# Block sums of an MLP weight matrix: added on VectorE, or by accumulating transfers on GpSimd's queue during the RWKV part

## The chip, the cores and the metric

The kernel runs on one core of a Trainium2 chip. TensorE (PE) multiplies matrices; its weight loads have a row of their own in the profile (PEld). VectorE (DVE), ScalarE (ACT) and GpSimd (POOL) work on tiles in the core's memory, and SyncE (SP) issues most of the transfers. POOL and ACT can issue transfers too. The metric is the device time of one execution in microseconds (us), as the median of several runs. Lower is better.

## The reference

One layer of a hybrid decoder runs on 512 new prompt tokens and 64 sample tokens (8 sequences of 8), so 576 rows of width 1024. RWKV-7 time mixing and differential attention run on the same normalised input and are merged by gates; then comes an MLP with a squared ReLU:

```python
xn = rmsnorm(x, lp['g_mix'], NORM_EPS)
P = xn @ lp['w_in']
...
o_a, S = rwkv7_branch(Pr, S0, lp)
...
m = gate_a * (o_a @ lp['w_br_a']) + gate_b * (o_b @ lp['w_br_b'])
x = x + m @ lp['w_out']
hn = rmsnorm(x, lp['g_ffn'], NORM_EPS)
x = x + jnp.square(jax.nn.relu(hn @ lp['w_up'])) @ lp['w_down']
```

`w_up` is 1024 x 4096 and `w_down` 4096 x 1024. Everything is float32. The outputs are the final rows, the new keys and values, the RWKV states and the last normalised rows.

## The kernel before

Activations are kept transposed: 128 channels on the partitions, 576 tokens on the free axis, cut into two halves of 288. Weights come in blocks of 128 x 128. To keep float32 accuracy, each operand is split into a rounded half `hi` (made by ACT) and a rest `lo` (made by DVE), and each product is three matmuls: hi times hi, hi times the rest of the other operand, and the reverse.

`stream` (called through `dense` and `finish`, or held as a generator) does this for one column block of a weight: `load` brings its raw rows on SP's queue into a ring of three buffers (tag "raw"), `halve` splits them into rings "hi" and "lo" of three, then for each half of the tokens and each k three matmuls follow, and an eviction closes each half. One such triple is the unit that the change counts.

The stages are, in the order of the program: Q, K and V of four heads (`qkv`), attention (`prompt`, `sample`), then the RWKV part (`rwkv`, `chain`), whose small, dependent steps leave holes on PE. These are filled with streams from a list `waiting`, by `fill` and `take`: 14 shifted projections (`shifted`, tile names z), 16 gates (`gate`, g, two blocks of 8) and 8 blocks of the attention's output projection (`branch_b`, brb, of 8 triples each where the others have 16). A gate ends with the store of its result to `gt_d` (line 452). After that come the RWKV branch's output projection (bra), the product with `w_out` (wo), and the MLP.

POOL's work in the RWKV part consists of small steps inside the chain (the powers `nr` and `var`, the copy `nb`, clearing `ST` and `TT`, the masked products `vm`), one clearing per shifted stream (`Z`), and stores of results (`out_Sp`, `out_Ss`, `oa_d`). The load of the sample states `s0` on SP (line 859) reuses a buffer that such a store reads.

The first MLP product is done in pairs of column blocks (`up_pair`). Weights and activations are seen as 2 x 2 blocks, and seven block products in place of eight are formed from sums of blocks. Sums of the activations (`t1` to `t4`) are made once, while `w_out` runs. The sums of the weights are made anew for every pair: `s12` holds a21 + a22 and that minus a11; `s34` holds a11 - a21 and a12 minus the second of `s12`. These are four DVE additions of 128 x 512. Then `halve` splits `s12`, the first row, `s34` and a22. `down` multiplies with `w_down` between the pairs.

The order on each engine isn't written out by hand. A planner orders instructions by priority as their inputs become ready in its own model of time. `prio(FEED + ...)` puts loads and halvings ahead of everything else on their engines, and `prio(FILL + ...)` orders the matmuls. What the planner has put in a queue is then executed in that order, and an instruction that waits holds up those behind it on its engine.

Of the kernel before, what the change touches and what calls it, by code (L numbers as in the profile page):

```python
# [8 lines left out]
F32 = mybir.dt.float32  # L9
F32R = mybir.dt.float32r  # L10
I32 = mybir.dt.int32
AF = mybir.ActivationFunctionType
# [3 lines left out]
P = 128  # L16
# [9 lines left out]
DFF = 4096  # L26
# [15 lines left out]
def tile_hybrid_step(ctx, tc, xT, xsT, ktab, vtab, s0T, ptab, w_in, vecs, w2a2, g2, lamv,  # L42
                     w_bra, w_brb, w_out, w_up, w_down, cst, bias_p, bias_s,
                     yT, kTo, vTo, Sp, Ss, sh):
    nc = tc.nc
# [9 lines left out]
    ring = {"job": 0}  # L55

    def act(out, in_, func=AF.Copy, **kw):
        ring["act"] = AE.activation(out=out, in_=in_, func=func, **kw)  # L58

    def tt(out, a, b, op, eng=None):  # L60
        ins = (eng or VE).tensor_tensor(out=out, in0=a, in1=b, op=op)  # L61
        if eng is None:
            ring["tt"] = ins

    def stt(out, a, s, b, op0, op1):
        VE.scalar_tensor_tensor(out=out, in0=a, scalar=s, in1=b, op0=op0, op1=op1)
# [4 lines left out]
    def mm(out, lhsT, rhs, start=True, stop=True):  # L71
        ring["mm"] = PE.matmul(out=out, lhsT=lhsT, rhs=rhs, start=start, stop=stop)  # L72
        return ring["mm"]
# [9 lines left out]
    FEED, LATE, FILL = -1000000, 500000, 1000000  # L83

    @contextmanager
    def prio(at):
        was, tc.cur_priority = tc.cur_priority, at
        yield
        tc.cur_priority = was

    MUL, ADD, SUB, MAX = ALU.mult, ALU.add, ALU.subtract, ALU.max
# [20 lines left out]
    c = const.tile([P, C_END], F32, name="cst_sb")  # L112
# [41 lines left out]
    def stream(src, kt, xh, xl, spans, evac, name, raws=None, together=False, banks=None,  # L154
               keep=None):


        his, los = [], []
        n = min(kt, ring["piece"])
        if src is None:  # L160

            job = ring["job"] = ring["job"] + 1
            raws = []
            his, los = ([t[:, k] for k in range(kt)] for t in keep)
        else:
            job, raws = raws or load(src, kt, name)

        def halve(i):
            raw = raws[i]
            with prio(FEED + 1000 * job + 100 if banks is None else FEED + 1001 + 40 * i + job):  # L170
                if keep:
                    hi, lo = (t[:, i * n:(i + 1) * n] for t in keep)
                elif banks is None or i == 0:
                    hi = ring["pool"].tile([P, n, P], F32R, tag="hi", name=f"hi_{name}_{i}")
                    lo = ring["pool"].tile([P, n, P], F32R, tag="lo", name=f"lo_{name}_{i}")
                else:
                    hi, lo = (zp.tile([P, NT], F32R, tag=f"Pt{job - 1}", name=f"{half}_{name}_{i}", bufs=2)[
                        :, :n * P].rearrange("p (k w) -> p k w", k=n) for half in ("hi", "lo"))
                act(hi, raw)
                tt(lo, raw, f32(hi), SUB)  # L180
                his.extend(hi[:, k] for k in range(n))
                los.extend(lo[:, k] for k in range(n))
        for i in range(len(raws)):
            halve(i)
        pss = banks or [psd.tile([P, 512], F32, tag="d", name=f"ps_{name}_{i}") for i in range(len(spans))]
        order = [(k, i) for i in range(len(spans)) for k in range(kt)]
        for k, i in sorted(order) if together else order:
            t0, w = spans[i]
            ps = pss[i]
            rh, rl = (x[k][:, t0:t0 + w] if isinstance(x, list) else x[:, k, t0:t0 + w] for x in (xh, xl))  # L190
            yield 1000 * job
            mm(ps[:, :w], his[k], rh, start=(k == 0), stop=False)
            yield 1000 * job
            mm(ps[:, :w], his[k], rl, start=False, stop=False)
            yield 1000 * job
            mm(ps[:, :w], los[k], rh, start=False, stop=(k == kt - 1))
            if k == kt - 1:
                with prio(FEED + 1000 * job + 200 + 20 * i):
                    evac(ps[:, :w], t0, w)
# [63 lines left out]
    oa_d = tc.dram_tile([HB, P, NT], F32, name="oa_d")  # L263
    ob_d = tc.dram_tile([HB, P, NT], F32, name="ob_d")
    gt_d = tc.dram_tile([2 * KT, P, NT], F32, name="gt_d")

    zp = pool("zp", stack=ph1)
    zw = pool("zw", 2, stack=ph1)
# [2 lines left out]
    with tc.tile_pool(name="xin", bufs=2, reuse_waits="tile") as xin:  # L271
# [6 lines left out]
        for k in range(0, KT, 4):  # L278
            for j in range(3):
                with prio(FEED + 1000 + 10 * k + j):  # L280
                    name = f"raw_{'qkv'[j]}0_{k}"
                    if k == 0:
                        raw = ring["pool"].tile([P, 4, P], F32, tag="raw", name=name, bufs=3)
                    else:
                        raw = zw.tile([P, 1 + NX], F32, tag="z" if j else "tz", name=name,
                                      bufs=2 if j else 1)[:, :4 * P].rearrange("p (k w) -> p k w", k=4)
# [841 lines left out]
    for i, d in enumerate((0, 4, 1, 5, 2, 6, 3, 7)):  # L1128
        xr = wt_.tile([P, NT], F32, tag="xr", name=f"xr{d}")
        with prio(FEED + 1000 * (ring["job"] + 1) - 1):  # L1130
            nc.sync.dma_start(out=xr, in_=xT[:, d])
        hf = hfs[d] = wt_.tile([P, NT], F32, tag="hf", name=f"hf{d}", bufs=3)
        k = d % 4

        def ev(ps, t0, n, d=d, k=k, xr=xr, hf=hf):
            x, h = ya[:, d, t0:t0 + n], hf[:, t0:t0 + n]
            tt(x, ps, xr[:, t0:t0 + n], ADD)
            act(h, x, scale=v(V_GF + d))
            if d < 4:
                if t0 == 0:  # L1140
                    put("b11", k, h)
                else:
                    t1 = wt_.tile([P, 288], F32, tag="t", name=f"t1_{k}", bufs=4)
                    tt(t1, h, hf[:, :288], SUB)
                    hfs["t1", k] = t1
                    put("t1", k, t1)
            elif t0:
                for n, x, y in (("t2", h, hfs["t1", k]), ("t3", h, hfs[k][:, 288:])):
                    t = hfs[n] = wt_.tile([P, 288], F32, tag="t", name=f"{n}_{k}", bufs=4)
                    tt(t, x, y, SUB)  # L1150
                    put(n, k, t)
                put("b22", k, h)
            else:
                put("b21", k, h)
                t4 = wt_.tile([P, 288], F32, tag="t", name=f"t4_{k}", bufs=4)
                tt(t4, h, hfs["t2"], SUB)
                put("t4", k, t4)
        dense(w_out[d], KT, mh, ml, HALF[::1 if d < 4 else -1], ev, f"wo{d}")

        for j, (t0, n) in enumerate(HALF):  # L1160
            o = acc[:, t0:t0 + n]
            if i == 0:
                act(o, ya[:, d, t0:t0 + n], AF.Square)
            else:
                sq = cbank(j, f"sq{d}{j}")[:, :n]
                act(sq, ya[:, d, t0:t0 + n], AF.Square)
                tt(o, o, sq, ADD)
# [12 lines left out]
    def up_pair(f1):  # L1180
# [2 lines left out]
        for f in (f1, f2):  # L1183
            qs[f] = hq_pool.tile([P, 2, NT], F32R, tag="q", name=f"q{f}")
        with prio(FEED + 1000 * (ring["job"] + 1)):
            rows = [sp_.tile([P, 2, 4, P], F32, tag="raw", name=f"a{f}", bufs=3) for f in (f1, f2)]
            for r, f in zip(rows, (f1, f2)):
                nc.sync.dma_start(out=r.rearrange("p i k w -> p (i k) w"), in_=w_up[f])
        (a11, a12), (a21, a22) = ([r[:, i] for i in range(2)] for r in rows)
        s12, s34 = (sp_.tile([P, 2, 4, P], F32, tag="s", name=f"s{i}_{f1}", bufs=2) for i in (12, 34))  # L1190

        def halve(x, two, after):

            pl = sp_ if two else ring["pool"]
            shape = [P, 2, 4, P] if two else [P, 4, P]
            hi, lo = (pl.tile(shape, F32R, tag=t + "2" * two, name=f"{t}{after}_{f1}", bufs=3)
                      for t in ("hi", "lo"))
            with prio(FEED + 1000 * (ring["job"] + after) + 100):
                act(hi, x)
                tt(lo, x, f32(hi), SUB)  # L1200
            return [(hi[:, i], lo[:, i]) for i in range(2)] if two else (hi, lo)

        with prio(FEED + 1000 * (ring["job"] + 1) + 90):
            tt(s12[:, 0], a21, a22, ADD)
            tt(s12[:, 1], s12[:, 0], a11, SUB)
        S1, S2 = halve(s12, True, 1)
        A11, A12 = halve(rows[0], True, 2)
        with prio(FEED + 1000 * (ring["job"] + 3) + 90):
            tt(s34[:, 0], a11, a21, SUB)
            tt(s34[:, 1], a12, s12[:, 1], SUB)  # L1210
        S3, S4 = halve(s34, True, 5)
        A22 = halve(a22, False, 7)

# [16 lines left out]
        def out(f, half, c, r=None):  # L1230

            sp = slice(288 * half, 288 * half + 288)
            r = c if r is None else r
            act(r, c, AF.Relu)
            act(r, r, AF.Square)
            act(qs[f][:, 0, sp], r)
            tt(qs[f][:, 1, sp], r, f32(qs[f][:, 0, sp]), SUB)
# [267 lines left out]
```

## Time and profile before

| | |
|---|---|
| median of 3 runs | 1002.25 us (1001.97 to 1002.99) |
| span of the profiled execution | 1004.0 us, 24422 instructions |
| PE, weight loads | 97%, 92% of the span |
| DVE, ACT, POOL | 69%, 50%, 9% |
| stages (us from the start) | Q, K, V and attention to about 165; RWKV with z, gates and brb to about 524; bra to 552; wo to 604; MLP to the end |

Nothing is shown of what lies around the profiled execution's span; it is 1.75 us above the median of the other runs. Times in the views below are us from the span's start, and instruction durations ns or us as marked. A row such as "L61 DVE TENSOR_TENSOR s<-a" names the line, the engine, the operation, and what is written from what. Most operations go through helpers, so many share one line and are told apart by their tiles. "SPq" and "POOLq" are the queues' own instructions.

### The profile page before, as it was taken

What the parts mean: (1) busy time and instruction counts of PE and PEld (TensorE: products, weight loads), DVE (VectorE), ACT (ScalarE), POOL (GpSimd) and SP (SyncE); (2) the same over time, 40 slices, a digit from 0 to 9 for tenths busy, and PEclk for the clock granted to TensorE, in tenths of its full rate; (3) what the DMA queues carried; (4) which work ended last, traced back from release to release, by engine and by line L of the source; (5) the groups of instructions that cost most, each with busy time, mean ns of one, the idle gap of its engine ahead of it and who ended that gap; (6) DMA issues with size and microseconds to landing.
All of it is one profiled execution on the core that took longest, in us unless ns stands there. A gap on an engine that the chain in (4) does not pass through costs nothing.

```text
span 1004.0 us, 24422 instructions
## 1 busy us (share of the span) xinstructions
PE 975.5 (97%) x10012; PEld 919.9 (92%) x10012; DVE 689.5 (69%) x1459; ACT 497.3 (50%) x1094; POOL 88.3 (9%) x171
## 2 busy tenths in 40 slices
PE   8999999899999999999999999999999999999996
PEld 8999998898887878888889999999999999999996
DVE  6698666774946669445588798966666666666744
ACT  6576555354435344443344666644444444444732
POOL 2511001301010340000300000000000000000001
PEclk9999999999989989999999999999999999999998
DMA  7312673121111225222377642222222222221402
GB/s 265 142 66 88 204 221 120 54 64 45 43 47 57 69 87 171 80 70 102 106 215 237 195 152 74 95 85 95 85 85 95 84 85 85 85 84 44 128 10 95
DMA packets 50833, 105.75 MB, mean 105 GB/s; under 512 B 6066, under 2 KB 8114, under 8 KB 50594
## 3 DMA queue, kind: packets, MB, share of 16 engines
q1 hardware_dynamic: 47442, 96.95, 30.2%
q0 software_dynamic: 1648, 5.35, 1.4%
q8 instruction: 79, 1.29, 0.5%
q10 hardware_dynamic: 1632, 1.89, 0.5%
q14 instruction: 32, 0.26, 0.1%
HBM read 89.38 MB, written 14.78 MB: 104 GB/s over the span
## 4 chain that ended last, share of the span: by engine, by line
PE 86%; DVE 6%; ACT 3%; DMA 2%; issue 2%; POOL 1%; SPq 0%; DVEq 0%; POOLq 0%; ACTq 0%
PE ps_dn L72 21%; PE ps_g L72 9%; PE ps_z L72 8%; PE ua L1224 5%; PE ux L1224 5%; PE ps_wo L72 4%; PE uc L1224 3%; PE ud L1224 3%; PE ub L1224 3%; PE ps_k L72 2%; PE ps_brb L72 2%; PE pch L72 2%; PE ps_q L72 2%; PE ps_v L72 2%; PE pA L72 2%
## 5 line engine op out<-in xcount | busy, mean ns | idle before, releaser
L72 PE MATMUL ps_dn<-q,hi_dn 128*128 128x288 f32 x768 | 154.7, 296 | 0.0
L72 PEld LDWEIGHTS ps_dn<-q,hi_dn 128*128 128x128 f32 x768 | 122.8, 188 | 1.5
L72 PE MATMUL ps_dn<-q,lo_dn 128*128 128x288 f32 x384 | 113.2, 295 | 0.0
L72 PE MATMUL ps_g<-xl,hi_g 128*128 128x288 f32 x256 | 80.2, 313 | 0.0
L72 PE MATMUL ps_g<-xh,lo_g 128*128 128x288 f32 x256 | 79.3, 310 | 0.0
L72 PE MATMUL ps_g<-xh,hi_g 128*128 128x288 f32 x256 | 79.2, 310 | 0.0
L72 PEld LDWEIGHTS ps_dn<-q,lo_dn 128*128 128x128 f32 x384 | 72.1, 188 | 0.0
L72 PE MATMUL ps_z<-xh,lo_z 128*128 128x288 f32 (+1 forms) x224 | 69.6, 311 | 0.0
L72 PE MATMUL ps_z<-xh,hi_z 128*128 128x288 f32 (+1 forms) x224 | 68.3, 305 | 0.0
L72 PE MATMUL ps_z<-xl,hi_z 128*128 128x288 f32 (+1 forms) x224 | 67.6, 302 | 0.0
L61 DVE TENSOR_TENSOR ya<-ya,ps_dn 128x288 f32<-128x288 f32 x96 | 43.4, 453 | 29.3 <-PE ps_dn L72 29.3
L58 ACT ACTIVATE hi_dn<-raw_dn 128x512 fp32r<-128x512 f32 x48 | 30.1, 628 | 57.0 <-PE ps_dn L72 57.0
L1224 PE MATMUL ua<-h_b,hi 128*128 128x288 f32 x256 | 53.2, 298 | 0.0
L1224 PE MATMUL ux<-h_t,hi 128*128 128x288 f32 x256 | 52.3, 296 | 0.0
L58 ACT ACTIVATE c<-c 128x288 f32<-128x288 f32 x112 | 48.4, 439 | 7.5 <-DVE c L61 5.8
L72 PEld LDWEIGHTS ps_g<-xh,hi_g 128*128 128x128 f32 x256 | 49.0, 191 | 2.9 <-issue 1.6
L72 PEld LDWEIGHTS ps_g<-xl,hi_g 128*128 128x128 f32 x256 | 49.0, 191 | 1.9
L72 PEld LDWEIGHTS ps_g<-xh,lo_g 128*128 128x128 f32 x256 | 49.1, 192 | 1.4
L58 ACT ACTIVATE hi<-a 128x1024 fp32r<-128x1024 f32 (+1 forms) x32 | 27.1, 846 | 42.0 <-PE ps_dn L72 34.3
L72 PE MATMUL ps_dn<-q,w 128*128 128x320 f32 (+1 forms) x336 | 46.4, 298 | 0.0
L61 DVE TENSOR_TENSOR lo<-s,hi 128x1024 fp32r<-128x1024 f32 x32 | 39.2, 1225 | 10.2 <-ACT hi L58 10.0
L72 PEld LDWEIGHTS ps_dn<-q,w 128*128 128x128 f32 x336 | 45.3, 190 | 0.1
(395 smaller groups left out, 2801.7 us busy)
## 6 DMA issues: line engine op xcount, KB each, us to landing
a<-in_w_up_dram SPq DMA_DIRECT2D x32, 512.0 KB, 3.3
raw_dn<-in_w_down_dram SPq DMA_DIRECT2D x64, 256.0 KB, 2.9
raw_g<-in_w_in_dram SPq DMA_DIRECT2D x32, 256.0 KB, 3.2
raw_z<-in_w_in_dram SPq DMA_DIRECT2D x28, 256.0 KB, 3.0
gt_d<-gg SPq DMA_DIRECT2D x16, 288.0 KB, 2.5
g<-gt_d SPq DMA_DIRECT2D x16, 288.0 KB, 3.7
kp<-in_ktab_dram SPq DMA_DIRECT2D x16, 256.0 KB, 4.0
vp<-in_vtab_dram SPq DMA_DIRECT2D x16, 256.0 KB, 3.7
```

The costliest lines, as they stand in the source:

```text
L58: ring["act"] = AE.activation(out=out, in_=in_, func=func, **kw)
L61: ins = (eng or VE).tensor_tensor(out=out, in0=a, in1=b, op=op)
L72: ring["mm"] = PE.matmul(out=out, lhsT=lhsT, rhs=rhs, start=start, stop=stop)
L1224: ring["mm"] = PE.matmul(out=ps[:, :288], lhsT=l[:, k], rhs=hb[blk][:, h, k], start=start and i == 0, stop=i == 11, skip_group_check=skip)
```

## The change

A new DRAM tile `us_d` takes four sums for each of the 16 pairs. They are made by transfers that POOL's queue issues: plain copies of blocks of `w_up`, and transfers that add onto what is there (`accum_op`). The signs are chosen so that only additions are needed: slot 0 holds a21 + a22, slot 1 a11 plus slot 0, slot 2 a11 + a21, slot 3 a12 plus slot 1. To make up for this, three of the activations' sums and the second column block of each pair change their signs.

`pace()` is called after every third matmul of a stream. From the 201st call on, each 16th call issues the next transfer, with an added dependency on the matmul issued last. Slots 1 and 3 get their addition one group later than their copy.

In `up_pair`, `s12` and `s34` are loaded from `us_d`, and of the second row only a22 is loaded, into the ring that `w_down` uses. The four DVE additions go. The buffers for raw rows are now five, and the two for sums go.

```diff
             mm(ps[:, :w], los[k], rh, start=False, stop=(k == kt - 1))
+            pace()
...
+    us_d = tc.dram_tile([DFF // 256, P, 4, 4 * P], F32, name="us_d")
+
+    def block_sums(n):
+
+        blk = w_up.rearrange("(g o) p (i k) w -> o i p g (k w)", o=2, i=2)
+        dst = us_d.rearrange("g p s c -> s p g c")
+        a11, a12, a21, a22 = (blk[o, i] for o in range(2) for i in range(2))
+        moves = [(0, a21, None, 0), (2, a11, None, 0), (1, dst[0], ADD, 1), (1, a11, None, 0),
+                 (3, a12, None, 0), (3, dst[1], ADD, 1), (0, a22, ADD, 0), (2, a21, ADD, 0)]
+        for g in range(0, DFF // 256 + n, n):
+            for s, src, op, late in moves:
+                at = slice(g - n * late, g - n * late + n)
+                if not 0 <= at.start < DFF // 256:
+                    continue
+                go = {} if op is None else {"accum_op": op}
+                with prio(FEED):
+                    dma = nc.gpsimd.dma_start(out=dst[s][:, at], in_=src[:, at], **go)
+                tc.add_manual_dep(dma.ins, ring["mm"].ins.name, mybir.DependencyInfo(
+                    mybir.DependencyClass.Sync, mybir.DependencyReason.DATA), reason="pace")
+                yield
+
+    def pace():
+        ring["n"] = ring.get("n", 0) + 1
+        if ring["n"] > 200 and ring["n"] % 16 == 0:
+            next(sums_, None)
+
+    sums_ = block_sums(4)
...
-                    tt(t1, h, hf[:, :288], SUB)
+                    tt(t1, hf[:, :288], h, SUB)
...
-                tt(t4, h, hfs["t2"], SUB)
+                stt(t4, hfs["t2"], -1.0, h, MUL, SUB)
...
-            rows = [sp_.tile([P, 2, 4, P], F32, tag="raw", name=f"a{f}", bufs=3) for f in (f1, f2)]
-            for r, f in zip(rows, (f1, f2)):
-                nc.sync.dma_start(out=r.rearrange("p i k w -> p (i k) w"), in_=w_up[f])
-        (a11, a12), (a21, a22) = ([r[:, i] for i in range(2)] for r in rows)
-        s12, s34 = (sp_.tile([P, 2, 4, P], F32, tag="s", name=f"s{i}_{f1}", bufs=2) for i in (12, 34))
+            s12, a1, s34 = (sp_.tile([P, 2, 4, P], F32, tag="raw", name=f"{n}{f1}", bufs=5)
+                            for n in ("s12", "a1", "s34"))
+            a22 = ring["pool"].tile([P, 4, P], F32, tag="raw", name=f"a22{f1}", bufs=3)
+            flat = lambda t: t.rearrange("p i k w -> p (i k w)")
+            nc.sync.dma_start(out=flat(s12), in_=us_d[f1 // 2, :, 0:2].rearrange("p s c -> p (s c)"))
+            nc.sync.dma_start(out=a1.rearrange("p i k w -> p (i k) w"), in_=w_up[f1])
+            nc.sync.dma_start(out=flat(s34), in_=us_d[f1 // 2, :, 2:4].rearrange("p s c -> p (s c)"))
+            nc.sync.dma_start(out=a22, in_=w_up[f2][:, 4:8])
...
-        with prio(FEED + 1000 * (ring["job"] + 1) + 90):
-            tt(s12[:, 0], a21, a22, ADD)
-            tt(s12[:, 1], s12[:, 0], a11, SUB)
         S1, S2 = halve(s12, True, 1)
-        A11, A12 = halve(rows[0], True, 2)
-        with prio(FEED + 1000 * (ring["job"] + 3) + 90):
-            tt(s34[:, 0], a11, a21, SUB)
-            tt(s34[:, 1], a12, s12[:, 1], SUB)
+        A11, A12 = halve(a1, True, 2)
         S3, S4 = halve(s34, True, 5)
...
-            act(r, c, AF.Relu)
+            act(r, c, AF.Relu, scale=-1.0 if f == f2 else 1.0)
```

More of the change, by code (lines that the diff above doesn't have):

```diff
@@ L1147, in ev @@
             elif t0:
-                for n, x, y in (("t2", h, hfs["t1", k]), ("t3", h, hfs[k][:, 288:])):
+                for n in ("t2", "t3"):
                     t = hfs[n] = wt_.tile([P, 288], F32, tag="t", name=f"{n}_{k}", bufs=4)
-                    tt(t, x, y, SUB)
+                    if n == "t2":
+                        stt(t, h, -1.0, hfs["t1", k], MUL, SUB)
+                    else:
+                        tt(t, h, hfs[k][:, 288:], SUB)
                     put(n, k, t)
```

## The prediction

> **What bounds the kernel now.** I read the page's busy table first, then the table of busy time by stage, then the chain of work that ended last, and last the places where TensorE (PE) stands idle in the stages that the change touches.
>
> ```profile
> PE 975.5 (97%) x10012; PEld 919.9 (92%) x10012; DVE 689.5 (69%) x1459; ACT 497.3 (50%) x1094; POOL 88.3 (9%) x171
> ...
> 113.00:552.00 439.00, 424.13 (x5938) 377.91 (x5937) 290.99 (x673) 196.39 (x467) 54.58 (x88) 0.98 0.34 109
> 552.00:568.00 16.00, 15.21 (x111) 14.52 (x110) 10.68 (x24) 8.70 (x20) 0.00 (x0) 1.00 0.62 205
> 568.00:655.00 87.00, 87.00 (x649) 85.99 (x650) 78.34 (x158) 57.11 (x128) 0.00 (x0) 1.00 0.37 114
> 655.00:965.00 310.00, 310.00 (x2303) 308.49 (x2302) 207.70 (x374) 153.09 (x288) 0.00 (x0) 1.00 0.26 84
> ...
> 737.61 12.89 PE ps_dn L72 x96
> 750.50 1.60 PE uc L1224 x12
> ```
>
> After the page's first row, the columns of the stage rows are: stretch, length, busy time of PE, weight loads, VectorE (DVE), ScalarE (ACT), GpSimd (POOL), granted clock, DMA share, GB/s. The stage that the change wants to relieve is the MLP (655 to 965): PE is busy 310 of 310 us at clock 1.00, DVE 208. The chain there is PE alone: twelve products of one block in 1.60 us, 96 of the second matrix in 12.89 us, so one matmul each 0.133 to 0.134 us, group after group. An engine that is busy two thirds of the time beside a PE with no hole is not the bound. In the stretch before (568 to 655) DVE is fuller, 78 of 87 us, but PE has no hole there either. The idle PE time is in the attention, RWKV and gate stages (113 to 552: 14.9 us), where the new transfers go.
>
> **What is removed.** Each of the 16 pairs of rows of `w_up` loses four DVE additions.
>
> ```profile
> L61 DVE TENSOR_TENSOR s<-a 128x512 f32<-128x512 f32 x16 | 11.0, 688 | 0.3 <-DMA a<-in_w_up_dram 0.3
> ...
> L61 DVE TENSOR_TENSOR s<-a,s 128x512 f32<-128x512 f32 x16 | 10.9, 684 | 0.0
> ...
> L66 DVE SCALAR_TENSOR_TENSOR ml<-g,mh 128x288 fp32r<-128x288 f32 x16 | 7.3, 454 | 0.6 <-ACT mh L58 0.5
> ...
> 562.79 0.69 DVE L61 TENSOR_TENSOR s<-a 128x512 f32<-128x512 f32 x1 [0.32 <-DMA a<-in_w_up_dram]
> ...
> 564.37 0.69 DVE L61 TENSOR_TENSOR s<-a,a 128x512 f32<-128x512 f32 x1
> ...
> 567.18 1.29 DVE L61 TENSOR_TENSOR lo_wo<-raw_wo,hi_wo 128x512 fp32r<-128x512 f32 x2
> ...
> 566.89 0.29 PE L72 MATMUL ps_wo<-ml,hi_wo 128*128 128x288 f32 x1
> 567.32 0.40 PE L72 MATMUL ps_wo<-mh,hi_wo 128*128 128x288 f32 x1
> 567.92 0.40 PE L72 MATMUL ps_wo<-mh,lo_wo 128*128 128x288 f32 x1 [0.20 <-DVE lo_wo L61]
> 568.16 0.29 PE L72 MATMUL ps_wo<-mh,hi_wo 128*128 128x288 f32 x1
> ```
>
> Four groups of 16 near 0.686 us are 43.9 us of DVE. In the MLP this is worth nothing: PE covers it and is the bound. One place pays: three of the first pair's additions stand ahead of the halving of the output matrix (`lo_wo` at 567.18), and PE waits for that. The four starts from 566.89 to 568.16 cover 1.27 us, where three steps at 0.134 are 0.40. Three additions in front are some 1.8 us of DVE, more than the 0.87 lost, so I take the whole hole: **-0.9 us**. What is late next there is PE itself. The changed signs (`stt` for `tt`, Relu with scale -1) swap equal operations on 288 columns, 0.454 us by the row above for this form; they count as nothing, as DVE and ACT both have room behind PE.
>
> **What is added: 32 transfers on POOL's queue.** `block_sums(4)` gives 4 copies and 4 additions for each of 4 groups, each over 4 pairs: 128 x 4 runs of 2 KB, 1 MB. The counter stands at 192 after the four heads' Q, K and V, so number 1 falls at the end of the first shifted stream (n = 208), 14 of them in the z streams, 13 in the gates to n = 624, the last (n = 704) at the end of the fourth `branch_b`. By the rows below that is near 125, then 288 to 448 for the gates and 508 us for the last. The first MLP loads come at 555: the sums are there in time, and the last group's are needed much later.
>
> ```profile
> 125.71 0.11 POOL L426 MEMSET Z<- 128x1 f32 x1 [6.01 <-DVE P L66]
> ...
> 288.34 0.33 SPq L452 DMA_DIRECT2D gt_d<-gg  x1
> ...
> 344.85 0.33 SPq L452 DMA_DIRECT2D gt_d<-gg  x1
> ...
> 359.07 0.33 SPq L452 DMA_DIRECT2D gt_d<-gg  x1
> ...
> 360.03 1.96 SPq L859 DMA_DIRECT2D s<-in_s0T_dram  x2
> ...
> 447.81 0.33 SPq L452 DMA_DIRECT2D gt_d<-gg  x1
> ...
> 508.63 0.32 SPq L483 DMA_DIRECT2D gt_d<-gb  x1
> ...
> L388 POOL DMA_DIRECT2D out_kTo_dram<-kT x4 | 2.2, 548 | 8.2 <-DVE kT L61 8.2
> ...
> L588 POOL DMA_DIRECT2D ob_d<-obh x4: 602/602/608, 72.2 to 169.2; - x4
> L711 POOL DMA_DIRECT2D ob_d<-obs x1: 797/797/797, 175.4 to 175.4; - x1
> ...
> q1 hardware_dynamic: 47442, 96.95, 30.2%
> ...
> raw_dn<-in_w_down_dram SPq DMA_DIRECT2D x64, 256.0 KB, 2.9
> ...
> bp<-in_bias_p_dram SPq DMA_DIRECT2D x1, 1024.0 KB, 7.2
> ```
>
> Issue: the trace has no transfer of this form, and the nearest is the store of `obs`, which also has 512 runs: 0.80 us on POOL. 32 x 0.8 = 26 us, on an engine that is busy 88 of 1004. Bounds: 0.55 (the 128-run stores) and, at four times the price for a second set of reads and longer runs, 3.2 us. I take 0.8.
>
> Transport: no transfer from DRAM to DRAM and no addition is in the trace. By the q1 row (96.95 MB in 30.2% of 1004 us) a MB costs all 16 engines 3.1 us; the 1 MB load of `bp` took 7.2 us in a crowded stretch. A copy lies between these; an addition reads twice, so from 3.1 to 14.4. I take 3.3 and 6.6: 16 x 3.3 + 16 x 6.6 = 158 us over some 385 us, which raises the DMA share there from 0.34 to about 0.75. Not below nothing: the transfers only add bytes.
>
> Most of this is covered. Where the halvings of the gates' weights waited longest, it was for PE to free their buffers, and no wait of theirs for a load is listed:
>
> ```profile
>   PE ps_g L72: 21.6, 16
> ...
> DMA to landing us min/median/max: 2.5/3.2/5.0
> ```
>
> Three raw buffers, each worth some 5 us of stream, hide a landing that grows from 3.2 to 6 or 8 us. The cover is thin at three places:
>
> ```profile
> 341.42 1.15 POOL L1037 DMA_DIRECT2D out_Sp_dram<-So  x2 [59.50 <-DVE So L69]
> 342.61 3.27 POOL L818 MEMSET ST<- 64x1152 f32 x3
> 345.97 3.56 POOL L61 TENSOR_TENSOR vm<-SVU,cst_sb 128x512 f32<-128x512 f32 x3
> ...
> PE pI L72 <- DMA s<-in_s0T_dram: 1.0, 1, 1.0
> ...
> 344.48 0.94 PE L72 MATMUL pA<-ST,KB 128*128 128x128 f32 x7
> ...
> PE pk L76 <- POOL nb L763: 2.7, 1, 2.7
> ```
>
> First, POOL from 341.4 to 349.5 works almost without a break (state stores, clearing of `ST`, masks `vm`), and PE needs the cleared `ST` at 344.5. The gate that ends by 344.85 brings a transfer there: 0.8 us, and about even odds that it comes ahead of work that PE needs: **+0.4**. Second, PE already waits 1.0 us for the load of `s0` (360.03), and the transfer of the gate that ends by 359.07 starts just before it. Two loads of 256 KB that share the engines half and half take 0.8 us longer each: **+0.8** (0 to 7, if an addition is all in front). Third, from 507 to 552 the DMA is full already:
>
> ```profile
> 507.00:524.00 17.00, 16.40 (x115) 15.60 (x116) 13.73 (x28) 8.50 (x23) 1.01 (x2) 1.00 0.80 248
> ...
> 533.73 4.83 DMA g<-gt_d
> ```
>
> The last addition lands in it and its 6.6 us exceed the 3.4 us that are free in that stretch; the rest moves the gate loads on the chain a little: **+0.4** (0 to 3). What else waits on POOL behind a transfer are the powers `nr` and `var`, the copy `nb`, the small clearings of `Z`, and the stores; PE waited for `nb` once, 2.7 us. Each such place has one meeting in about ten, and I add nothing.
>
> In the MLP, SP loads 1.75 MB a pair in four issues in place of 1 MB in two. 12 MB more are 39 us of DMA over 350, on a share of 0.26, and 32 issues of 0.33 us on a queue that mostly waits for buffers. The quarter row `a22` takes a slot of the ring of three that the second matrix uses; its loads still lead by three slots of 3.2 us against a landing of 2.9. Nothing, with PE as cover; without it, some tenths per pair.
>
> **Sum:** -0.9 + 0.4 + 0.8 + 0.4 = +0.7 us: the profiled execution's span would go from 1004.0 to 1004.7, and the median of the runs, 1002.25 and so 1.75 below that span, to **1003.0**.
>
> A page's rule on the issue: the Trainium skill, SBUF — State Buffer, section "SBUF: two separate sides", says that GpSimd cannot write the descriptors of its transfers while VectorE runs in a two-port mode, and gives about 620 ns alone against 3100 beside such a copy. By that an issue would cost 0.8 + 2.5 = 3.3 us (my estimate from this page) and the first of the three terms 1.6 in place of 0.4. No run here shows such a stretching: the four stores of `obh` took 602 to 608 ns beside whatever DVE ran.
>
> **Rivals.** *A wait on POOL takes the place of the sums (slower, 0.20).* The transfer does not only take its issue time, it stands in POOL's queue until its matmul is done. If the planner puts the transfer for 344.85 ahead of the state stores at 341.42, POOL stands until the gate's last matmul near 343.4; clearing `ST` then starts 2.0 + 0.8 later, and `pA` and all behind it. The second pair's state stores and masks are a second such place: 2 x 2.8 = 5.6, with the other terms as above without the +0.4, gives +5.9: 1008.2; one place gives 1005.4. It decides as soon as one transfer stands ahead of such an item. For it: POOL waited 59.5 us in one piece, so its order is fixed long before. Against it: the transfer becomes ready earlier by PE's own order.
>
> *The transfers collide with loads (slower, 0.10).* At the upper price, 14.4 us an addition, the load of `s0` comes some 4 us later and the last gates' loads 2 us: -0.9 + 0.4 + 4 + 2 = +5.5, 1007.8. It decides where an addition is under way at 360. The Trainium skill, DMA: Bandwidth & Descriptors, section "Issuing engines are not separate DMA queues", speaks for this: transfers from any engine run on the same 16 engines and interleave. No run here has the two streams together.
>
> *DVE was more in the way than PE's busy time shows (faster, 0.13).* From 568 to 655 weight loads are busy 85.99 of 87 us, so up to 1.0 us may be lost there, and of the 0.79 us that PE idles from 552 to 568 only 0.20 stand at the hole, which leaves 0.6. With the 0.9 that is -2.5 and no cost: 999.8. Against it: PE's own row is full.
>
> *The sums come too late* would need a delay of over 40 us from 508; I put it inside the rest.
>
> **Chances.** Forecast 0.57, the rivals 0.20, 0.10 and 0.13. A measurement of this kernel can tell about 0.2%, or 2 us, from no change. So faster 0.13, within 0.57, slower 0.30. The range holds 8 in 10: below, most of the third rival; above, one place of the first and nearly all of the second: 1000.2 to 1007.5.
>
> **What would show it.** The four `s` rows are gone and DVE drops by about 44 us, with the MLP stretch as long as now. The gap at 567 is gone. The new POOL rows show near 0.8 us each; 3 us would refute the issue term. The wait of `pI` for `s0` near 1.8 us confirms the second term. A shift of `pA` past 347 shows the first rival, an addition that takes over 10 us to land the second. A stage before 552 that gets shorter by more than 1 us would be something that I have no mechanism for, and would make the prediction wrong.

## The result, and the profile after

| | before | after |
|---|---|---|
| median | 1002.11 us (1001.88 to 1002.99, 4 runs) | 1035.36 us (1034.79 to 1037.09, 4 runs) |
| span of the profiled execution | 1004.0 us | 1033.0 us |

The changed kernel is slower: the ratio is 1.0333, with a 95% interval of 1.0319 to 1.0348. The forecast was 1003.0, and the range ended at 1007.5. The first rows are from the page of the changed kernel.

```profile
span 1033.0 us, 24530 instructions
...
PE 987.4 (96%) x10012; PEld 930.0 (90%) x10012; DVE 656.5 (64%) x1395; ACT 498.3 (48%) x1094; POOL 120.5 (12%) x203
...
DMA  7312796564735459355697773344333333331302
```

The 64 additions are gone from DVE (1459 to 1395 instructions, 689.5 to 656.5 us), POOL has 32 instructions more, and PE has the same 10012 matmuls. DVE's busy time fell by 33 us and not by the 44 of the four rows, because instructions overlap in it: the sum of their durations fell from 762 to 719 us. The DMA row (tenths of 16 engines, in slices of 25.8 us) stands at 4 to 9 in most slices from the fifth to the 24th. The stage table of the same kernel, for the MLP, which now begins 30 us later:

```profile
685.00:995.00 310.00, 310.00 (x2303) 308.53 (x2302) 182.72 (x328) 152.78 (x287) 0.00 (x0) 1.00 0.35 111
```

PE is busy 310 of 310 us with 2303 matmuls, exactly as before, and DVE 183 in place of 208: the MLP neither gained nor lost. All that was lost lies ahead of it. The transfers of the changed kernel (queue rows: packets, MB, share of 16 engines; issue rows: count, KB each, median us from issue to landing):

```profile
q1 hardware_dynamic: 52050, 109.53, 32.3%
q0 software_dynamic: 14448, 38.90, 16.4%
...
us_d<-in_w_up_dram POOLq DMA_DIRECT2D x24, 1024.0 KB, 8.0
...
us_d<-us_d POOLq DMA_DIRECT2D x8, 1024.0 KB, 10.8
raw_g<-in_w_in_dram SPq DMA_DIRECT2D x32, 256.0 KB, 5.4
...
ob<-ob_d SPq DMA_DIRECT2D x4, 288.0 KB, 10.2
s<-in_s0T_dram SPq DMA_DIRECT2D x4, 256.0 KB, 8.3
```

POOL's queue (q0) rose from 1.4% to 16.4%. The load of `s0` now lands in 8.3 us (4.1 before), that of `ob` in 10.2 (4.6 before). The table of PE's waits shows what that did (us in total, times, longest):

```profile
PE ps_bra L72 <- DVE g L66: 4.9, 6, 1.8
PE pI L72 <- DMA s<-in_s0T_dram: 4.7, 1, 4.7
PE pW L72 <- issue: 4.6, 3, 2.1
PE pZ L72 <- issue: 3.7, 3, 2.7
PE pZ L72 <- ACT W L58: 3.2, 1, 3.2
```

The wait for `s0` was 1.0 us before. The others are new or grown: `g` in the gate stage, a product `W` that ACT makes too late, and "issue", time in which PE waits for no semaphore at all. The timeline of the changed kernel shows who came in the way (start, duration, engine, line, and in brackets the idle time ahead):

```profile
350.94 0.77 POOL L283 DMA_DIRECT2D us_d<-in_w_up_dram  x1 [0.33 <-PE pch L72]
351.75 1.05 POOL L846 MEMSET ST<- 64x1152 f32 x1
...
365.81 1.33 POOL L283 DMA_DIRECT2D us_d<-us_d  x1 [0.33 <-PE ps_g L72]
...
368.13 0.33 SPq L887 DMA_DIRECT2D s<-in_s0T_dram  x1
...
407.82 1.29 ACT L58 ACTIVATE obh<-ob 128x576 fp32r<-128x576 f32 x2 [6.05 <-DMA ob<-ob_d]
```

A transfer's issue stands ahead of a clearing of `ST`. An adding transfer of 1 MB starts 2.3 us ahead of the `s0` load. And ACT waits 6.05 us for `ob` in its queue, with the `W` of the RWKV chain behind it: PE's wait for `W` is a load's lateness, passed on through an engine that executes in order.

### The profile page after: what moved, and what is told of

Read it like the earlier page. It is cut to its first block, busy times and chain, and to the rows that moved or that the text cites. A ratio compares the mean times of both kernels' runs of the same rounds, so it can differ in the third digit from the quotient of the medians.

```text
span 1033.0 us, 24530 instructions
## 1 busy us (share of the span) xinstructions
PE 987.4 (96%) x10012; PEld 930.0 (90%) x10012; DVE 656.5 (64%) x1395; ACT 498.3 (48%) x1094; POOL 120.5 (12%) x203
## 3 DMA queue, kind: packets, MB, share of 16 engines
q0 software_dynamic: 14448, 38.90, 16.4%
## 4 chain that ended last, share of the span: by engine, by line
PE 82%; DVE 7%; DMA 5%; ACT 3%; issue 2%; POOL 1%; SPq 0%; DVEq 0%; ACTq 0%; POOLq 0%
PE ps_dn L72 20%; PE ps_g L72 9%; PE ps_z L72 8%; PE ua L1252 5%; PE ux L1252 5%; PE ps_wo L72 3%; PE ps_k L72 3%; PE uc L1252 3%; PE ud L1252 2%; PE ub L1252 2%; PE ps_q L72 2%; PE pch L72 2%; PE ps_v L72 2%; DMA s<-in_s0T_dram 1%; PE pA L72 1%
## 6 DMA issues: line engine op xcount, KB each, us to landing
us_d<-us_d POOLq DMA_DIRECT2D x8, 1024.0 KB, 10.8
```

## The experiments

Four explanations were held against each other: foreign packets ahead of loads that are needed at once (A in the expectations); waiting and issuing on POOL's queue, the prediction's first rival; the new loads of the MLP; and bytes that cost the same wherever they lie (D). A fifth came up on the way: foreign packets ahead of the fetches of PE's instructions (F). "Foreign" are the packets of the new transfers, seen from any other transfer. Ratios are to the kernel before on the same chip. In all kernels with transfers but the seventh and the eighth the sums in `us_d` aren't used (in some they aren't fully made) and the MLP makes its own on DVE, as before.

**One: the kernel before, with the transfers of the change and nothing else of it.**

```diff
+            pace()
...
+    sums_ = block_sums(4)
```

> Only the RWKV part of the change: the 32 transfers as they are, but the MLP makes its sums on VectorE as before, and nobody reads us_d. Theory A (the bytes of the transfers delay other loads, so the cost arises before 580 us) and theory B (the waiting and issuing on GpSimd's queue holds up the chain) both expect 1030 to 1036 us, with the load of s0, the load of ob and the output projection of RWKV as late as after the change. Theory C (the MLP's loads from us_d are what costs) expects 1002 to 1004.

1033.28 us, ratio 1.0332 (1.0296 to 1.0368): the whole loss, with the MLP unchanged. So the MLP's new loads are out as a cause. PE's matmuls stand in the same order as before, so the two traces can be laid on each other step by step, a step being the time from the start of one matmul to the start of the next. The last matmul starts 28.0 us later. Of these, 4.0 us arise in the one step ahead of the first product behind `s0`, 3.6 in two steps behind the first `ob`, 6.2 in the gate stage, and 6.3 in single steps of small products, mostly `pZ` and `pW`, of up to 2.4 us each. Another 7.0 us are spread over steps that changed by less than 0.25 us each, in which PE's granted clock is halved in one of the two traces only.

**The halved clock** is a part of the loss that none of the explanations named. The row is from the changed kernel's stage table (granted clock 0.93); below it, the same eight products before and after:

```profile
400.00:447.00 47.00, 42.16 (x977) 38.03 (x978) 26.02 (x51) 19.38 (x46) 3.74 (x7) 0.93 0.58 179
...
394.45 1.13 PE L72 MATMUL pA<-ST,KB 128*128 128x128 f32 x8
410.74 2.04 PE L72 MATMUL pA<-ST,KB 128*128 128x128 f32 x8 [0.71 <-DVE ST L61]
```

From 409.9 to 416.7 us the granted clock is 0.50, and the eight products take 2.04 us in place of 1.13. Between 100 and 600 us it is 0.50 for 37.4 us in the changed kernel and for 17.0 before; 20.4 us more at half speed are a loss of at most some 10 us. In the changed kernel such a stretch begins close to the end (0.8 us ahead to 1.5 us behind) of each of the six waits of PE of 1.8 us or more. That a wait brings the lower clock with it is inferred from this order, and it is no fixed rule: in a second profile of the kernel before (experiment ten), waits of 2.7 and 1.8 us had no such stretch behind them.

**Two: the same 32 transfers, waits and 512 runs, each run 128 bytes in place of 2 KB.**

```diff
-                    dma = nc.gpsimd.dma_start(out=dst[s][:, at], in_=src[:, at], **go)
+                    dma = nc.gpsimd.dma_start(out=dst[s][:, at, :32], in_=src[:, at, :32], **go)
```

> As the run above, with the same 32 transfers at the same places with the same waits and 512 runs each, but runs of 128 bytes in place of 2 KB, so 64 KB in place of 1 MB. Theory A expects most of the cost gone: 1002 to 1006, and landings of s0 and ob near 4 to 5 us again. Theory B expects it to stay: over 1025, since the waits and the issue time on GpSimd are the same.

1005.52 us, ratio 1.0058 (1.0042 to 1.0075):

```profile
ob<-ob_d SPq DMA_DIRECT2D x4, 288.0 KB, 4.1
s<-in_s0T_dram SPq DMA_DIRECT2D x4, 256.0 KB, 4.1
```

`s0` and `ob` land in 4.1 us again. POOL is as busy as with the full transfers (121 us). So its waits and issues cost at most 4 to 7.5 of the 33 us, and the bytes the rest.

**Three: every addition turned into a plain copy. Four: the 16 copies alone, no additions.**

```diff
-                go = {} if op is None else {"accum_op": op}
+                go = {}
```

```diff
+                if op is not None:
+                    yield
+                    continue
```

> As the first run, with every transfer a plain copy, so the adding and its second read go and the bytes written stay. If the adding is what is dear (landing 10.8 us against 8.0 for those that read w_up), theory A expects about half of the cost: 1014 to 1020. If a MB costs the same either way, 1028 to 1035. Theory B expects no change against the first run.

> As the first run, with the 16 adding transfers left out and the 16 copies at their places. The bytes written are halved. Theory A expects a third to a half of the cost, 1010 to 1018, depending on which of the critical loads still meets a transfer: the one near 366 us before s0 is an adding one and would be gone, so s0 near 5 us. Theory B expects half of it by count: 1016 to 1020, with s0's wait unchanged only if the wait on GpSimd made it.

1018.28 us (ratio 1.0162, 1.0132 to 1.0192) and 1009.85 (1.0082, 1.0058 to 1.0106): within A's range and just below it, and outside what the waits on POOL's queue would give. The rows of POOL's queue, of the first experiment and then of the third, give the transport of each form:

```profile
q0 software_dynamic: 14448, 38.90, 16.3%
...
q0 software_dynamic: 10352, 38.90, 11.4%
```

With 32 copies q0 takes 11.4% of 1020.7 us, so a copy of 1 MB costs all engines 3.2 us (without the 1.4% of before). In the first experiment q0 takes 16.3% of 1032.2 us, 52 us more, so an addition costs 3.2 us more than a copy, or 6.4. The time rises faster than the engine time at the end: by the ratios 8, 16 and 33 us for 51, 102 and 154 us of it. With the copies alone `s0` and `ob` land as before (3.4 and 4.0 us). In its profiled execution (1015.89 us, the longest of five) PE's largest new waits are those for issue (`pZ` 6.0, `pW` 2.6 us).

**Five: the same bytes in 128 transfers of 256 KB.**

```diff
-        if ring["n"] > 200 and ring["n"] % 16 == 0:
+        if ring["n"] > 200 and ring["n"] % 4 == 0:
...
-    sums_ = block_sums(4)
+    sums_ = block_sums(1)
```

> The transfers of the change in quarters: 128 transfers of 256 KB, each behind every fourth triple of matmuls, the same bytes in the same stretch, not used later. Theory A (what counts is how long one transfer of 1 MB stands in the way of a load that meets it): a load meets at most 2 to 3 us of foreign packets at a time, s0 lands in 5 to 6 us, and the time is 1010 to 1022 us. Theory D (the total of engine time taken counts, however it is cut): the meetings are four times as many and a quarter as long, and the time stays at 1030 to 1037 us. A rise above 1037 would be the price of 96 more issues and waits on POOL (96 times 0.8 us, 77 us more of POOL).

1047.05 us, ratio 1.0436 (1.0391 to 1.0481): worse, and not better as A had it. The rows are of its transfers, then of its waits.

```profile
us_d<-in_w_up_dram POOLq DMA_DIRECT2D x96, 256.0 KB, 5.2
...
ob<-ob_d SPq DMA_DIRECT2D x4, 288.0 KB, 7.5
s<-in_s0T_dram SPq DMA_DIRECT2D x4, 256.0 KB, 5.1
```

```profile
PE pZ L72 <- issue: 9.4, 6, 3.8
...
PE pk L76 <- POOL nb L791: 4.0, 1, 4.0
PE pF L72 <- POOL vm L61: 2.7, 1, 2.7
```

The loads land sooner than with 1 MB transfers (`s0` 5.1 us, `ob` 7.5), but a quarter of the bytes still takes 5.2 us to land in place of 8.0, so a foreign transfer is in flight more of the time. The same bytes also take more of the engines (19.1% of 1045 us on q0, 185 us without the 1.4% of before, for 154), and POOL's own work (`nb`, `vm`) is now late behind 128 issues. How much of the loss is each isn't separated. Cutting a transfer up doesn't take it out of the way.

**Six: the same 32 transfers in the MLP.** This tells A from D.

```diff
-        if ring["n"] > 200 and ring["n"] % 16 == 0:
+        if ring["n"] > 928 and ring["n"] % 8 == 0:
```

> The same 32 transfers of 1 MB, not used later, each behind a matmul of the MLP in place of the RWKV part. Theory A (they are dear where a small load is asked for and needed within 4 us, which the RWKV part does at s0, ob and the gates, while the weights of the MLP are asked for well ahead): 1000 to 1006 us, the RWKV part as before (ua first at 606), with weights landing later (2.9 to 6 us or more) and no PE wait for them. Theory D (158 us of all engines cost 30 us wherever they lie, through instruction fetches and contention): over 1015 us, with PE waits spread through the MLP.

1006.33 us, ratio 1.0042 (1.0025 to 1.0059). The stage table's row for the MLP, then transfers, then the first wait:

```profile
655.00:965.00 310.00, 306.07 (x2259) 302.84 (x2259) 204.28 (x370) 150.84 (x285) 29.32 (x28) 1.00 0.67 181
```

```profile
us_d<-in_w_up_dram POOLq DMA_DIRECT2D x24, 1024.0 KB, 11.8
a<-in_w_up_dram SPq DMA_DIRECT2D x32, 512.0 KB, 5.7
```

```profile
PE ps_dn L72 <- DVE ya L61: 3.9, 5, 1.1
```

At a DMA share of 0.67 the weights land in 5.7 us (3.3 before) and PE still runs 306 of 310 us. All 32 were issued between 639 and 837 us and land in some 12 us each, so one is in flight nearly all of that time. The same bytes cost 4.7 us here and 33 in the RWKV part. D falls: it isn't the bytes alone, it is whom they meet. A isn't quite right either: it expected 1006 at most and no wait of PE, and PE waits 3.9 us for `ya`.

**Seven: the changed kernel whole, its transfers moved away from the loads of `s0`, `ob` and the gates.**

```diff
-        if ring["n"] > 200 and ring["n"] % 16 == 0:
+        if ring["n"] in (*range(208, 496, 12), *range(568, 680, 14)):
```

> The changed kernel whole, with the matmuls that release the transfers chosen anew: 24 of them every 12 triples from the 208th to the 484th, 8 every 14 from the 568th to the 666th, so that none is in flight at the load of s0 (360 us of before), at the loads of ob (385 to 407) and in the stage of the gates behind 523 us. Theory A: the jumps of 3.9, 3.5 and 2.6, and 6.2 us at those three places go, and the time is 1035.4 less 16, about 1019 us, perhaps some us more where the transfers now lie closer together. Theory D: the same bytes cost the same, 1033 to 1037 us. If it should come below 1002, the change would be worth having with another placing, which neither theory expects.

1023.69 us, ratio 1.0214 (1.0184 to 1.0245). Transfers, then waits:

```profile
ob<-ob_d SPq DMA_DIRECT2D x4, 288.0 KB, 4.4
s<-in_s0T_dram SPq DMA_DIRECT2D x4, 256.0 KB, 3.7
```

```profile
PE pZ L72 <- issue: 10.6, 7, 2.7
PE pW L72 <- issue: 4.2, 2, 2.6
```

Both loads land as before, and the waits for `s0`, `W` and `g` are gone from the head of the list. Laid on the changed kernel's trace, PE gains 4.8 us at `s0`, 3.9 at `ob` and some 8 in the gate stage, and loses about half of it again at `pZ` and `pW`, where the transfers now lie closer together. Laid on the trace of before, 13.8 of the 19.4 us that are left arise in single steps of the small products, and 7.6 in small steps at the halved clock (40.8 us of it between 100 and 600); the other places together gain 2. The table's 14.8 us of waits for issue are what is left to explain.

**What "issue" is.** A group of the small products is cut in its middle, where nothing can be waited for. Timeline of the kernel before:

```profile
292.52 0.60 PE L72 MATMUL pZ<-W,Y 32*32 32x32 f32 x47
293.94 0.34 PE L72 MATMUL pZ<-W,Y 32*32 32x32 f32 x17 [0.82 <-issue]
```

Its stage table in two stretches of 20 us, one of 40, and then the row of one queue for these 40 us in the table of transfers:

```profile
200.00:220.00 20.00, 19.54 (x170) 18.55 (x169) 15.26 (x35) 10.96 (x25) 0.40 (x4) 1.00 0.18 53
220.00:240.00 20.00, 19.46 (x576) 17.68 (x574) 10.23 (x22) 5.69 (x10) 0.20 (x2) 1.00 0.17 57
...
400.00:440.00 40.00, 38.94 (x1159) 35.11 (x1160) 19.18 (x42) 16.65 (x42) 0.00 (x0) 1.00 0.24 73
```

```profile
q8 instruction: 9, 0.15, 1.7%
```

Where the chain's 32x32 products run, PE executes 576 matmuls and 574 weight loads in 20 us, against 170 and 169 in a quiet stretch. In the 40 us from 400 the queue "instruction" brings nine packets of 16 KB while PE executes 1159 + 1160 instructions, 258 for each packet. Over the whole execution it is 79 packets for 20205 recorded instructions of PE. So PE's program comes by DMA, a packet every 4.4 us here.

The traces show that it is these packets that PE waits for. Take every step of over 0.35 us inside a group of the 32x32 products, without a semaphore, in the twelve traces: there are 67. Counted in PE's recorded instructions from the start, all 67 stand at the same place, 193 or 194 behind a multiple of 256. And in all 67 PE goes on 1.2 to 1.6 us after the end of a packet of this queue. A packet that is late thus stops PE where one block of its program ends. The next two experiments ask whether the new transfers make it late.

**Eight: the changed kernel whole, its transfers only where PE runs long matmuls and no small load is urgent. Nine: the kernel before, with ten transfers, all in the dense stretches, none at an urgent load.**

```diff
-        if ring["n"] > 200 and ring["n"] % 16 == 0:
+        if ring["n"] in (*range(92, 340, 14), 384, 398, 412, 450, 462, 474, *range(604, 680, 10)):
```

```diff
-        if ring["n"] > 200 and ring["n"] % 16 == 0:
+        if ring["n"] in (352, 362, 426, 434, 442, 566, 574, 582, 590, 598):
```

> The changed kernel whole, its 32 transfers released where PE runs long matmuls and no small load is needed at once: 18 between 52 and 222 us of before, 3 from 247, 3 from 306, 8 between 449 and 520; none where PE runs some 580 instructions in 20 us (220 to 245, 280 to 300, 400 to 445 us), none at the loads of s0, ob and the gates. Theory A+F (the cost is what meets a small load, and what meets a fetch of PE's instructions where PE uses them up fast): with placing apart from the loads the kernel took 1023.7 us, with 14.8 us of issue stalls of pZ and pW in its profile where before has about 1 to 3; without these it is 1005 to 1013 us. Theory D (the bytes cost as such inside the RWKV part): 1022 to 1036 us.

> The kernel before with 10 transfers (the first ten, not used later) and all of them in the stretches that the kernel named above leaves free: from 222, 280 and 411 us of before, where PE runs some 580 instructions in 20 us and no load of s0, ob or the gates is under way. Theory A+F: the waits of pZ and pW for issue grow by 1 to 2.5 us a transfer, 10 to 20 us, so 1012 to 1022 us, more than the 32 transfers placed in quiet stretches cost. Theory D: 10 of 32 transfers, a third of 33 us, about 1012 us at most, and with no special place for issue. A time within 1000 to 1006 would mean that dense stretches are no more sensitive than others.

1013.61 us with 32 transfers (ratio 1.0129, 1.0106 to 1.0153) and 1019.06 with ten (1.0168, 1.0138 to 1.0198). By the medians a transfer costs 0.4 us in a quiet place and 1.8 in a dense one, although half of the 32 and only three of the ten are additions. D, with no special place for issue, falls a second time. Waits of the eighth kernel, then of the ninth, then the ninth's timeline:

```profile
PE psb L72 <- DMA kp<-in_ktab_dram: 3.2, 1, 3.2
PE pZ L72 <- issue: 2.9, 3, 2.4
```

```profile
PE pZ L72 <- issue: 5.8, 3, 2.7
PE pW L72 <- issue: 3.9, 2, 2.1
```

```profile
292.17 0.74 POOL L283 DMA_DIRECT2D us_d<-in_w_up_dram  x1 [5.16 <-PE ps_g L72]
...
297.25 0.60 PE L72 MATMUL pZ<-W,Y 32*32 32x32 f32 x47
...
300.58 0.34 PE L72 MATMUL pZ<-W,Y 32*32 32x32 f32 x17 [2.73 <-issue]
```

The group is cut behind the same 47th matmul as before, and the hole is 2.73 us in place of 0.82, with a copy under way since 292.2. By the single packets of the ninth trace, the instruction packet ahead of the hole ran from 298.3 to 299.2, and PE went on 1.3 us after it; before, it ran from 291.6 to 292.5, and PE went on 1.4 us after it. The packet itself takes as long as before (0.94 and 0.93 us). It starts later: 4.3 us, and before 2.3, after PE passed the place 256 instructions earlier. Quiet places aren't free either: the eighth kernel met the loads of the key tables (`kp`, 3.2 us), and the rest of its 12 us is spread over small waits whose cause stays open.

**Ten: the kernel before, profiled once more.**

> The kernel before, unchanged: its profiled execution was 1004.0 us where its runs have a median near 1002 and one of 1000.2. A second profile tells how far two executions of the same program lie apart, and with that how much of the small differences (the 128-byte transfers at 1005.5) can be read from single traces. Every theory expects 1000 to 1003 us, the same waits of PE and the same landings (s0 4.1, ob 4.6 us).

1002.35 us. Its page and its waits:

```profile
span 1000.6 us, 24422 instructions
```

```profile
PE pZ L72 <- issue: 1.0, 3, 0.4
PE ps_g L72 <- issue: 0.7, 1, 0.7
PE pW L72 <- issue: 0.5, 1, 0.5
```

Two executions of one program differ by 3.4 us in their spans, most of it where the clock differs: between 100 and 600 us the first has 17.0 us at a granted clock of 0.50 and the second 6.8, and steps in which only one of the two has it make up 4.1 us. So terms below 1 us can't be read from one pair of traces, and a sum over a trace is uncertain by some 4 us.

No version here beats the kernel before. With PE busy 310 of 310 us in the MLP on both sides, the sums on DVE cost nothing that a better placing could win back.

## Why the prediction was wrong

**Right: where nothing is won.** The four `s` rows, 44 us, are gone and the MLP is as long as before, 310 us of PE in 310. The hole behind `lo_wo` at 567 is gone, but wo's matmuls take no less time from the first start to the last (52.7 us against 52.4): PE has other small waits there. The -0.9 didn't come, and it wouldn't have mattered.

**Right: the price of a transfer.** Predicted were 3.3 us of all engines for a copy and 6.6 for an addition; measured are 3.2 and 6.4. The sum of 158 us stands against q0's (16.4% - 1.4%) of 1033, 155 us. The issue term, 0.8 us, held for the copies (0.74 to 0.83 us on POOL) and was low for the additions (1.24 to 1.34). The rule of the Trainium skill, SBUF — State Buffer, section "SBUF: two separate sides", by which the prediction made it 3.3 us, didn't show: no issue of the changed kernel took longer than 1.342 us. Whether VectorE ran in a two-port mode beside one of them, the trace doesn't tell.

**Wrong: "Most of this is covered", with +0.8, +0.4 and +0.4 for three places.** This is the step that failed: the path from the transfers to PE. By landing times, 24 x 8.0 + 8 x 10.8 us in flight are 278 of the 412 us between the first issue (123.7) and the last (535.2), so a load or fetch in that stretch meets a transfer about two times in three (their packets move for 214 us). The prediction had both factors, 32 transfers and 7.2 us for the nearest load of 1 MB, and used the transport for the mean DMA share and two loads alone. (Its "one meeting in about ten" was for POOL's small steps behind an issue; the second experiment leaves at most 7.5 us for those.) In the changed kernel, PE's last matmul starts 29.0 us later, and this is where it arises:

- `s0`: +0.8 predicted, from two loads that share the engines half and half. Measured is a wait of 4.7 us for 1.0 before, with an adding transfer issued 2.3 us ahead of the load. The place was right and the size wrong; experiment seven, with nothing in flight there, lands it in 3.7 us.
- `ob`: not named at all. ACT's 6.05 us wait became PE's 3.2 for `W`; 3.9 us in the matched traces.
- the gate stage: +0.4 predicted; 4.9 us of waits for `g`, and 6.3 us in the matched traces.
- clearing `ST`: +0.4 predicted; an issue did come ahead of a clearing, and PE fell back by no more than 0.7 us between 300 and 355 us of before.
- PE's instructions: no term at all. The idle time that the profile calls "issue" was not asked about. It is 8.3 us of `pZ` and `pW` in the changed kernel against 2.3 before, and 14.8 in the seventh, which runs 12 us faster; 6.1 us in the matched traces.
- the clock: no term at all. 7.4 us in small steps outside the gate stage, where PE runs at half the clock in one of the two traces only.

**The rivals.** The second, "the transfers collide with loads", was the mechanism, at a chance of 0.10 and a price of 5.5 us for two places. It asked for an addition under way at `s0` and named an addition that takes over 10 us to land as its sign; both came (10.8 us). But it priced meetings at two loads, and the case has them at `ob` and at PE's instructions as well, and the lower clock on top. The rule that it cited, the Trainium skill, DMA: Bandwidth & Descriptors, section "Issuing engines are not separate DMA queues", agrees with the runs: transfers issued by POOL slow the loads that SP issues (`s0` 4.1 to 8.3 us), and with 128-byte runs they don't (4.1). The first rival, a wait on POOL ahead of its work, didn't decide: with all its waits in place the second experiment stands at 1005.5. That leaves it at most 4 to 7.5 of the 33 us, a size near its price of 5.6 us for two places; how much of it is POOL's waits and how much the small transfers themselves stays open. Its sign, `pA` past 347, came (351.5) without it: PE was already 6.9 us late at 300. The third, that DVE was in the way, is refuted: 25 us less DVE in the MLP moved nothing there.

Shown by runs: that the loss lies in the RWKV part (one), in the bytes (two), in where they lie (six, seven, eight, nine). Shown by the traces: that "issue" in the small products is a wait for the next block of PE's program (the same place in all 67 cases, 1.2 to 1.6 us behind a packet's end). Inferred, and not shown by a run of its own: that PE's longer waits bring the halved clock. Whether a late instruction packet waits in an engine's queue or at the memory stays open; its own transfer isn't longer.

## What to carry to other kernels

Before moving work from an idle-looking engine's time to the DMA engines, work out how much of the stretch the new transfers are in flight (count times landing time), and take that share as the chance that each urgent small load meets one: a mean DMA share of 0.34 says nothing about that. Count PE's program among the small loads where its instructions are short. Put bulk transfers where loads run several buffers ahead and PE's instructions are few and long; the same 32 MB cost 4.7 us in such a stage and 33 in the chain of small dependent steps. And relief for an engine that stands beside a PE without holes is worth nothing, so any cost decides.

## What the hardware showed that was not expected

- PE's program competes with the data. It takes a 16 KB packet for each 256 instructions or so (79 for 20205), and where PE runs 32x32 products it stops at the end of a block: 0.82 us before, 2.73 at the same matmul with a copy in flight. The Trainium skill, Runtime: NRT & Kernel Launch, section "Instruction fetch mechanics", gives 256 instructions for each block and a DMA queue of the sequencer's own, which agrees; it calls the cost of crossing a block mostly hidden, and here it was not, even before the change.
- A transfer's size isn't its standing in the way: 256 KB transfers took 5.2 us to land against 8.0 for 1 MB, so four quarters are in flight longer than the whole, and by the ratios the kernel was 10 us slower than in the first experiment, part of which may be POOL's lateness.
- An accumulating transfer from DRAM to DRAM took 10.8 us to land where both sides are the new tile (7.1 as a plain copy in the third experiment), and costs the engines twice a copy (6.4 against 3.2 us a MB) and POOL 1.24 to 1.34 us to issue in place of 0.74 to 0.83.
- The granted clock of PE fell to 0.50 for 37.4 of 500 us in the changed kernel and for 17.0 and 6.8 us in two executions of the kernel before, mostly close behind waits of PE. If the waits bring it, a wait costs more than its own length; that is inferred.
